# Two-phase depthwise convolution with three half filters, in a two-layer trunk on one core

## The chip, the cores and the metric

The kernel runs on one core of one Trainium2 chip. The metric is the device time of one execution in microseconds (us). The profile names the engines PE (TensorE, matmul; PEld is its weight load), DVE (VectorE), ACT (ScalarE), POOL (GpSimd) and SP (SyncE, which issues the DMAs).

## The reference

Two layers of a trunk with 128 context tokens and 512 latent tokens (640 in all), width 1024. A layer normalises x, modulates it by a vector c (one for the context, one for the latent tokens), projects it to four groups of heads, mixes each group over the tokens (differential attention "da", latent attention "mla", neighbourhood attention "na", a Conformer convolution), projects back, adds, and then does the same around an MLP of 4096. The group that matters here:

```python
def conformer_conv(u, dw, db, ln_g, ln_b):
    a, b = jnp.split(u, 2, axis=-1)
    g = a * jax.nn.sigmoid(b)
    y = lax.conv_general_dilated(g, dw[:, None, :], window_strides=(1,),
                                 padding=[(CONV_W // 2, CONV_W // 2)], ...
                                 feature_group_count=CONV_CH) + db
    return jax.nn.silu(layernorm(y, ln_g, ln_b))

def modulation(cvec, w_mod, b_mod):
    m = jax.nn.silu(cvec) @ w_mod + b_mod
```

CONV_W is 31, CONV_CH is 256: each of 256 channels has its own filter of 31 taps along the tokens. The layernorm behind it runs over the 256 channels. The modulation is a product of a vector with a 1024 x 6144 matrix, for two vectors and two layers.

## The kernel before

**Number format.** Everything is float32. A matmul is made of three (mm3, L242 to L246): operands are split into a high part (rounded, by ACT, L192) and a low part (the rest, by POOL or DVE, L193), and high x high, high x low and low x high are summed in PSUM. So each weight granule costs splits on ACT and POOL before PE can use it. POOL takes its instructions in order.

**Memory.** The transposed x, the weights and all scratch lie in regions of one SBUF tile (`fa`), addressed by name. Two regions matter: "conv" (10,960 bytes a partition: the padded inputs g and the outputs y of the convolution, in two halves of 128 channels) and "c" (8192 bytes: the vectors silu(c) spread over all partitions, the row form `cb`, which VectorE needs when it computes modulation products itself). PSUM has two single banks g (`gb`) and three double ones s (`sb`).

**Stages.** start() loads x, computes silu(c), builds the row form of c by 16 PE transposes (L1223) and four DVE copies out of PSUM (L1241), sums the squares of x (L1235), computes layer 0's first modulation by dot products on PE (L1263), and runs the convolution's input projection as the normalised x arrives (L1284, L1289). Then, in each layer: the na value projection, na queries and keys, the da value projection (in_v, 40 groups of three matmuls of 288 columns, 120 in all), and a pipeline of 60 attention units (20 na, 20 da, 20 mla) with the other projections in between. The MLP follows (ff); during it VectorE computes the next layer's modulation from `cb` (mod_dot, L301).

**The convolution.** conv_evac writes g (L520 through a transposing view: the latent tokens are stored by grid column; L523 for the context). g is a row of 700 elements: 512 latent and 128 context tokens with zeros between. conv_taps (L413) makes 31 DVE instructions over 670 elements for each half: L419 multiplies by tap 0 and adds the bias, L423 multiplies by tap j and adds. They are background jobs: each has a price in ns (450 or 780), each piece of the program brings a credit (fill, L253), and when the credit covers the first job it is written into the program there. What is left is written out at attention unit DR = 2 (drain). Behind the last tap stands the chain conv_finish (L431): the sum of the two halves on POOL (L438), three ticks later a matmul with ones on PE (L443, mean over the channels), the subtraction of the mean on DVE (L446), squares on ACT (L451), their sum on POOL (L452), six ticks later again ones, and so on. A tick is a step of the program text: prices and ticks decide in which place of each engine's queue the instruction stands, not when it runs.

Of the kernel before, what the change touches and what calls it, by code (L numbers as in the profile page):

```python
# [11 lines left out]
AF = mybir.ActivationFunctionType  # L12
ALU = mybir.AluOpType
# [3 lines left out]
T = 640  # L17
# [11 lines left out]
C_BMOD, C_GMIX, C_GFF, C_DW, C_DB = 0, 48, 56, 64, 126  # L29
# [40 lines left out]
BGP = (100,100,100,100,100)  # L70
# [2 lines left out]
XPOS = 8  # L73
LEADF = (2,3,4,5,6,7)
YOUT = ((2,4,6,8),(2,4,6,8))
CB = "DDDD"
KINDS = ("D", "D")
ROWS = (1,1,0,0)
END = object()
# [3 lines left out]
class Builder:  # L83
# [310 lines left out]


    def conv_g(self, c):
        return self.F("conv", 2800 * c, 700)

    def conv_y(self, c):
        return self.F("conv", 5600 + 2680 * c, 670)  # L400

    def conv_zero(self):
        for c in range(2):
            g = self.conv_g(c)
            for a, b in ((0, 15), (527, 557), (685, 700)):
                self.nc.gpsimd.memset(g[:, a:b], 0.0)

    def conv_cols(self, l):
        nc = self.nc
        nc.vector.tensor_scalar(out=self.F("dwh", 0, 62), in0=self.col(l, C_DW, 62), scalar1=0.5, scalar2=None, op0=ALU.mult)  # L410
        nc.vector.tensor_scalar(out=self.F("lnh", 0, 4), in0=self.col(l, C_LNG, 4), scalar1=0.5, scalar2=None, op0=ALU.mult)

    def conv_taps(self, l, c):  # L413
        nc = self.nc
        g, y = self.conv_g(c), self.conv_y(c)
        dwh = self.F("dwh", 0, 2, 31)

        def first():
            nc.vector.tensor_scalar(out=y, in0=g[:, 0:670], scalar1=dwh[:, c, 0:1],  # L419
                                    scalar2=self.col(l, C_DB + c), op0=ALU.mult, op1=ALU.add)  # L420

        def tap(j):
            nc.vector.scalar_tensor_tensor(out=y, in0=g[:, j:j + 670], scalar=dwh[:, c, j:j + 1],  # L423
                                           in1=y, op0=ALU.mult, op1=ALU.add)
        self.bg.append((450, first, BGP[l]))
        for j in range(1, 31):
            self.bg.append((780, lambda j=j: tap(j), BGP[l]))
        if c == 1:
            self.bg.append((0, lambda: self.chain(self.conv_finish(l, (self.R("oa", 0, 2, T), self.R("oa", 5120, 2, T)))), 0))

# [77 lines left out]
    def conv_evac(self, l, c, part):  # L508
        nc = self.nc

        def evac(h, ps):
            t0, t1 = HALF[h]
            if part == "b":
                self.tabled(nc.scalar.activation(self.F("conv", 5600 + 2680 * c, T)[:, t0:t1], ps[:, 0:t1 - t0], AF.Tanh, scale=0.5))
                return
            th = self.F("conv", 5600 + 2680 * c, T)
            g = self.conv_g(c)
            nl = min(t1, NLAT) - t0
            out = g[:, 15:527].rearrange("p (r w) -> p w r", r=8)[:, t0 // 8:(t0 + nl) // 8]
            nc.vector.scalar_tensor_tensor(out=out, in0=th[:, t0:t0 + nl].rearrange("p (w r) -> p w r", r=8), scalar=1.0,  # L520
                                           in1=ps[:, 0:nl].rearrange("p (w r) -> p w r", r=8), op0=ALU.add, op1=ALU.mult)
            if t1 > NLAT:
                nc.vector.scalar_tensor_tensor(out=g[:, 557:685], in0=th[:, 512:640], scalar=1.0,  # L523
                                               in1=ps[:, nl:t1 - t0], op0=ALU.add, op1=ALU.mult)
                self.conv_taps(l, c)
        return evac
# [658 lines left out]
    def start(self):  # L1185
        nc, d = self.nc, self.d
        self.table(TABLE_TANH)
        ct = self.F("sq", 0, 8, 2)
        nc.sync.dma_start(ct, d["ct"])
        nc.scalar.dma_start(self.F("ident", 0, 256), d["cst"][:, 1024:1280])  # L1190
        for l in range(L):
# [1 line left out]
        ring = [self._view(self.at, 4096 * s, (1024,)) for s in range(4)] + [self.F("e", 4096 * s, 1024) for s in range(3)]  # L1193
        ring += [self.R(r, a, 1024) for r, a in (("oa", 4096), ("ob", 0), ("ob", 4096))]
        rows = [self.F("conv", 1024 * s, 256) for s in range(2)]
        self.ct, self.sel = ct, self.F("sq", 64, 2)
        sel = self.sel
        js = [w * 8 + k for k in range(8) for w in (SC1, SH1)]
        n = len(ring)
        self.ng = 4  # L1200
# [8 lines left out]
        for _ in range(4):  # L1209
# [5 lines left out]
                                       op0=ALU.add, op1=ALU.mult)  # L1215
        th = self.small(4 * 4).rearrange("p (a b) -> p a b", b=2)
# [1 line left out]
        self.table(TABLE_LN)  # L1218
        nc.vector.tensor_scalar(out=th, in0=th, scalar1=0.5, scalar2=0.5, op0=ALU.mult, op1=ALU.add)
        nc.vector.tensor_tensor(out=ct, in0=ct, in1=th, op=ALU.mult)  # L1220
        for v in range(2):
            for k in range(8):
                nc.tensor.transpose(self.sb[1 + v][:, k * 128:k * 128 + 128], ct[:, k, v:v + 1].to_broadcast([128, 128]), self.ident)  # L1223
        seq = ((0, 0, NLAT), (1, NLAT, T))
        ps = [self.gb[1][:, 0:NLAT], self.sb[0][:, 0:T - NLAT]]
        first = 0 if SUMS[0] == "D" else 1
        bufs = [self.F(*p, T) for p in (("tmp", 0), ("tmp", 3072), ("mla", 6144), ("conv", 8192))]
        for k in range(8):
            sq = bufs[k % 4]
# [3 lines left out]
            if k % 2 or SUMS[k // 2] == "D":  # L1233
                for v, a, b in seq:
                    nc.tensor.matmul(ps[v], self.ones, sq[:, a:b], start=k == first, stop=k == 7)  # L1235
        for v in range(2):
            for j, a in enumerate((0, 512)):
                if CB[2 * v + j] == "A":
                    nc.scalar.copy(self.cb[:, v, a:a + 512], self.sb[1 + v][:, a:a + 512])
                else:  # L1240
                    nc.vector.tensor_copy(self.cb[:, v, a:a + 512], self.sb[1 + v][:, a:a + 512])  # L1241
        for v, a, b in seq:
            self.rsq(self.rn[:, a:b], ps[v], 1.0 / 1024)
        pm = self.gb[0][:, 0:32].rearrange("p (a b) -> p a b", b=2)
# [2 lines left out]
        ws = [self.w_get(128) for _ in range(4)]  # L1247
# [73 lines left out]
        for i in range(4):  # L1321
# [2 lines left out]
            self.w_done()  # L1324
            evs[i](1, acb[i])
        self.table(TABLE_LN)

    def mod_rows(self, l, whichs):

# [74 lines left out]
    def mix(self, l):  # L1404
        nc, d = self.nc, self.d
        if l == 0:
            self.start()
        else:
            self.conv_zero()
            self.conv_cols(l)  # L1410
            self.in_conv(l, self.lead)
        self.swap(l, "bt")
        self.lam(l)
        for kind in range(3):
            self.na_bias_load(l, 0, kind)
        self.in_v(l, "na")
        for p in range(2):
            nc.sync.dma_start(self.qk_k("na", p)[:, 512:640], d["cnak"][l, :, p])
            self.mtile(self.na_evac(l, p, "q"))
            self.mtile(self.na_evac(l, p, "k"))  # L1420
        self.finish_chains()
        self.edge_load(0)
        self.edge_load(1)
        self.in_v(l, "da")
        self.ring = self.gb

        def rest():
            for p in range(2):
                nc.sync.dma_start(self.qk_k("da", p)[:, 512:640], d["cdak"][l, :, p])
                yield from self.pieces(self.da_evac(l, p, "q"))  # L1430
                yield from self.pieces(self.da_evac(l, p, "k"))
            yield from self.in_mla(l)
        plan = [(PL[0], PL[1], rest(), 14), (PL[15], PL[16], self.out_pieces(l, ["oa"], 2, 4), 16), (PL[3], PL[4], self.kv_up(l), 10), (PL[5], PL[6], self.out_pieces(l, ["ob"], 2, 4), 16),
                (PL[7], PL[8], self.q_up(l), 10), (PL[9], PL[10], self.out_pieces(l, ["oa"], 2, 4), 16),
                (PL[13], PL[14], self.ff_lead(l), 8)]
        hooks = {PL[2]: lambda: self.da_cut(1), PL[11]: lambda: self.chain(self.da_stack(1, 0)),
                 PL[12]: lambda: self.chain(self.da_stack(1, 1))}
        hooks[DR] = self.drain
        hooks[60] = lambda: self.swap(l, "we")
        self.out, self.out_n, self.norm_a = self.out_pieces(l, ["ob"], 2, 4, last=True), 0, self.norm(l, 1, 0)  # L1440
        plan = [[0, 0, *p] for p in plan]
        for t in self.pipeline(l, hooks):
            for job in [j for j in plan if t >= j[2]]:
                done, pos, t0, t1, gen, n = job
                if pos == 0 and t0 == PL[9]:
                    self.finish_chains("da")
                pos += 1
                while done < n and done * (t1 - t0) * 3 < pos * n:
                    next(gen)
                    done += 1  # L1450
                job[:2] = done, pos
# [244 lines left out]
```

## Time and profile before

| | |
|---|---|
| median of 3 runs (lowest to highest) | 1734.57 us (1733.45 to 1736.35) |
| profiled execution | 1735.52 us, span 1733.6 us |
| PE, DVE, ACT, POOL busy in the span | 96%, 62%, 43%, 38% |

The span runs from the first to the last instruction of the profiled execution. The trace allows a look at each instruction's start, duration and, where an engine stood idle ahead of it, what released it ("[8.73 <-POOL ra L193]": idle for 8.73 us until POOL's L193 had written ra).

### The profile page before, as it was taken

The numbers are of one execution on the slowest core, as the hardware profiler recorded it, in microseconds if no ns is written. First come the engines' busy times: TensorE is split into PE (matmuls) and PEld (weight loads), VectorE is DVE, ScalarE is ACT, GpSimd is POOL, SyncE is SP. The second block draws the span as 40 slices with busy tenths as digits, with TensorE's granted clock in tenths as the row PEclk, the third lists the DMA queues.
The fourth block names the chain that finished last, engine by engine and source line by source line (L and its number), as shares of the span: only waits on it lengthen the run. The fifth ranks groups of instructions, "written<-read, shape, count | busy, mean of one in ns | idle before, by whom it ended". The sixth has DMA issues, their size and how long they took to land. (4 is left out here: it accounts for less than half of the span.)

```text
span 1733.6 us, 29318 instructions
## 1 busy us (share of the span) xinstructions
PE 1664.6 (96%) x11368; PEld 1570.3 (91%) x11368; DVE 1083.0 (62%) x2136; ACT 740.7 (43%) x1655; POOL 656.5 (38%) x527
## 2 busy tenths in 40 slices
PE   7999999999989999999999899999999999999997
PEld 5869988788889999999999888887989999999997
DVE  4772448868988887876377933886784333333335
ACT  4323666756423332222343247776563322332322
POOL 0225533305344455544324364332343333333330
PEclk8999999999989999999999999999999999999999
DMA  9563244202355454443222222430113222222221
GB/s 367 185 202 106 75 110 101 63 14 86 110 160 167 147 158 147 152 153 111 73 71 71 64 86 84 108 88 20 50 39 97 73 74 74 80 79 74 74 62 61
DMA packets 62331, 178.28 MB, mean 103 GB/s; under 512 B 8656, under 2 KB 20048, under 8 KB 62192
## 3 DMA queue, kind: packets, MB, share of 16 engines
q1 hardware_dynamic: 61984, 176.14, 33.0%
q8 instruction: 89, 1.46, 0.3%
q14 instruction: 50, 0.41, 0.1%
q10 hardware_dynamic: 144, 0.13, 0.0%
q0 software_dynamic: 64, 0.14, 0.0%
HBM read 158.52 MB, written 3.83 MB: 94 GB/s over the span
## 5 line engine op out<-in xcount | busy, mean ns | idle before, releaser
L193 POOL TENSOR_TENSOR ra<-fa,ra 128x512 fp32r<-128x512 f32 (+1 forms) x239 | 345.7, 1459 | 545.2 <-ACT ra L192 524.5
L193 POOL TENSOR_TENSOR we<-fa,we 128x512 fp32r<-128x512 f32 x126 | 188.8, 1510 | 275.2 <-ACT we L192 253.5
L1077 DVE TENSOR_TENSOR fr<-fr 128x384 f32<-128x384 f32 (+1 forms) x128 | 103.9, 814 | 273.7 <-ACT or L1076 150.6
L192 ACT CAST ra<-fa 128x512 fp32r<-128x512 f32 (+1 forms) x240 | 147.2, 621 | 255.1 <-PE s L245 163.7
L244 PE MATMUL s<-ra 128*128 128x256 f32 (+2 forms) x600 | 185.4, 309 | 8.3 <-DVE fa L392 7.6
L245 PE MATMUL s<-ra 128*128 128x256 f32 (+2 forms) x600 | 184.3, 307 | 0.0
L246 PE MATMUL s<-ra 128*128 128x256 f32 (+2 forms) x600 | 184.1, 307 | 0.0
L301 DVE CUSTOM_DVE_ANT_0 fa<-fa 128x1024 f32<-128x1024 f32 x112 | 173.2, 1546 | 0.2
L392 DVE SCALAR_TENSOR_TENSOR fa<-s,fa 128x128 f32<-128x128 f32 (+1 forms) x310 | 121.3, 427 | 74.8 <-PE s L246 74.8
L246 PE MATMUL g<-ra 128*128 128x384 f32 (+2 forms) x508 | 158.3, 312 | 8.7 <-POOL ra L193 8.7
L244 PE MATMUL g<-ra 128*128 128x384 f32 (+2 forms) x508 | 162.2, 319 | 2.5 <-DVE bt L1010 1.9
L245 PE MATMUL s<-ra,we 128*128 128x384 f32 (+1 forms) x480 | 152.1, 317 | 12.0 <-DVE ra L370 12.0
L245 PE MATMUL g<-ra 128*128 128x384 f32 (+2 forms) x508 | 157.8, 311 | 0.8 <-POOL ra L193 0.8
L192 ACT CAST we<-fa 128x512 fp32r<-128x512 f32 x132 | 81.2, 620 | 175.2 <-PE s L245 127.9
L246 PE MATMUL s<-ra,we 128*128 128x384 f32 (+1 forms) x480 | 150.1, 313 | 0.0
L244 PE MATMUL s<-ra,we 128*128 128x384 f32 (+1 forms) x480 | 148.8, 314 | 0.8 <-DVE fa L520 0.8
L392 DVE SCALAR_TENSOR_TENSOR fa<-g,fa 128x128 f32<-128x128 f32 (+1 forms) x266 | 109.3, 441 | 40.4 <-PE g L246 39.0
L244 PEld LDWEIGHTS s<-ra 128*128 128x128 f32 x600 | 115.6, 193 | 17.6 <-DVE fa L392 7.9
L423 DVE SCALAR_TENSOR_TENSOR fa<-fa 128x670 f32<-128x670 f32 x120 | 124.1, 1098 | 0.5
L697 PE MATMUL g<-at 128*128 128x128 f32 x848 | 116.9, 277 | 2.8 <-DVE fa L392 1.5
L245 PEld LDWEIGHTS s<-ra 128*128 128x128 f32 x600 | 115.9, 193 | 4.0 <-issue 4.0
L246 PEld LDWEIGHTS s<-ra 128*128 128x128 f32 x600 | 115.8, 193 | 3.6 <-issue 3.6
(299 smaller groups left out, 4484.4 us busy)
## 6 DMA issues: line engine op xcount, KB each, us to landing
fa<-in_wg SPq DMA_DIRECT2D x187, 512.0 KB, 3.6
fa<-in_wmod SPq DMA_DIRECT2D x73, 512.0 KB, 4.2
at<-in_wmod SPq DMA_DIRECT2D x20, 512.0 KB, 6.5
ra<-ra SPq DMA_DIRECT2D x64, 96.0 KB, 2.2
ra<-ra SPq DMA_DIRECT2D x64, 80.0 KB, 2.3
fa<-in_nab SPq DMA_DIRECT2D x24, 192.0 KB, 3.7
fa<-in_xT SPq DMA_DIRECT2D x8, 320.0 KB, 5.9
os<-in_wmod SPq DMA_DIRECT2D x3, 512.0 KB, 10.2
```

The source lines that it names most:

```text
L192: nc.scalar.copy(hi, src)
L193: (lo_eng or nc.gpsimd).tensor_tensor(out=lo, in0=src, in1=hi.bitcast(F32), op=ALU.subtract)
L244: nc.tensor.matmul(out, a[0], b[0], start=start, stop=False)
L245: nc.tensor.matmul(out, a[0], b[1], start=False, stop=False)
L246: nc.tensor.matmul(out, a[1], b[0], start=False, stop=stop)
L301: self.nc.vector.tensor_tensor_reduce(out=self.junk, in0=slot, in1=self.cb[:, v], scale=1.0, scalar=0.0, op0=ALU.mult, op1=ALU.add, accum_ ...
L392: self.mark = nc.vector.scalar_tensor_tensor(out=xs, in0=ps[:, a - t0:b - t0], scalar=self.mod(l, v, which)[:, m:m + 1], in1=xs, op0=ALU.m ...
L423: nc.vector.scalar_tensor_tensor(out=y, in0=g[:, j:j + 670], scalar=dwh[:, c, j:j + 1], in1=y, op0=ALU.mult, op1=ALU.add)
L697: self.nc.tensor.matmul(u["o"], v[:, p * 128:p * 128 + 128] if v.shape[1] > 128 else v, u["pt"][:, b * 128:b * 128 + 128], start=b == 0, s ...
L1077: nc.vector.tensor_tensor(out=r, in0=r, in1=r, op=ALU.mult)
```

## The change

A convolution with 31 taps at even and odd positions is written with three half filters. For a half of the channels g is read in two phases, the words 0, 2, 4, ... (ph[0]) and 1, 3, 5, ... (ph[1]). The 16 even taps run over ph[0] into a_ (336 elements), the 15 odd taps over ph[1] into b_ (335), and 16 taps with the sums of neighbouring coefficients (`both`, and the last even tap alone) run over u = ph[1] + ph[0] shifted, into r, from which b_ is taken away at once. The outputs at even places are a_ + b_ + bias, those at odd places r + bias less a_ shifted. That makes 50 instructions of half the length for each half of the channels instead of 31, priced 350 (300 for a plain multiplication). y is written in the place of g. The even and odd taps read with a step of two words, the two combinations write with one; the taps on u read adjacent words.

The scratch u, r, b_ and `both` lies in region "c", where `cb` stood from the start on. So the row form of c is no longer built in start(): a new function c_rows does it at attention unit 41 of layer 0's pipeline, through the banks g. `ct` (silu(c) by columns) moves into the same region's end, a PSUM tile is cleared on DVE at the start, and conv_cols has one more addition per layer (the sums of neighbouring coefficients).

```diff
     def conv_g(self, c):
-        return self.F("conv", 2800 * c, 700)
+        return self.F("conv", 5344 + 2808 * c, 702)
     def conv_y(self, c):
-        return self.F("conv", 5600 + 2680 * c, 670)
+        return self.conv_g(c)[:, 0:670]
...
     def conv_taps(self, l, c):
         nc = self.nc
-        g, y = self.conv_g(c), self.conv_y(c)
...
-        self.bg.append((450, first, BGP[l]))
-        for j in range(1, 31):
-            self.bg.append((780, lambda j=j: tap(j), BGP[l]))
+        g, y, w, both = self.conv_g(c), self.conv_y(c), self.F("dwh", 0, 2, 31)[:, c], self.F("c", 5376, 2, 15)[:, c]
+        ph = [g[:, a:a + 701:2] for a in range(2)]
+        a_, u, r, b_ = (self.F("conv", 2560 * c, 336), self.F("c", 0, 350), self.F("c", 1408, 335),
+                        self.F("c", 2752 + 1344 * c, 335))
+        bias = self.col(l, C_DB + c)
...
+                    job(350, nc.vector.scalar_tensor_tensor, out=out, in0=src[:, i:i + n], scalar=x, op0=ALU.mult, **kw)
+                else:
+                    job(300, nc.vector.tensor_scalar, out=out, in0=src[:, 0:n], scalar1=x, scalar2=None, op0=ALU.mult)
+        even, odd = ([w[:, j:j + 1] for j in range(a, 31, 2)] for a in range(2))
+        job(350, nc.vector.tensor_tensor, out=u, in0=ph[1][:, 0:350], in1=ph[0][:, 1:351], op=ALU.add)
+        taps(a_, ph[0], even, 336)
+        taps(b_, ph[1], odd, 335)
+        taps(r, u, [both[:, j:j + 1] for j in range(15)] + [even[15]], 335, in1=b_, op1=ALU.subtract)
+        job(350, nc.vector.scalar_tensor_tensor, out=y[:, 0:670:2], in0=a_[:, 0:335], scalar=bias, in1=b_, op0=ALU.add, op1=ALU.add)
+        job(350, nc.vector.scalar_tensor_tensor, out=y[:, 1:670:2], in0=r, scalar=bias, in1=a_[:, 1:336], op0=ALU.add, op1=ALU.subtract)
...
-        ct = self.F("sq", 0, 8, 2)
+        ct = self.F("c", 7168, 8, 2)
...
+        nc.vector.memset(self.sb[2], 0.0)
...
-        for v in range(2):
-            for k in range(8):
-                nc.tensor.transpose(self.sb[1 + v][:, k * 128:k * 128 + 128], ct[:, k, v:v + 1].to_broadcast([128, 128]), self.ident)
...
+    def c_rows(self):
+
+        for v in range(2):
+            for b in range(2):
+                ps = self.g()
+                for k in range(4):
+                    self.nc.tensor.transpose(ps[:, k * 128:k * 128 + 128],
+                                             self.ct[:, 4 * b + k, v:v + 1].to_broadcast([128, 128]), self.ident)
+                self.nc.vector.tensor_copy(self.cb[:, v, 512 * b:512 * b + 512], ps)
...
+        if l == 0:
+            hooks[41] = self.c_rows
```

Lines of the changed kernel have other numbers: L243 to L245 are its L244 to L246, L192 its L193, L455 is the first ones matmul (L443 before), L458 the subtraction of the mean (L446), L778 the first maximum of an na unit (L766), L698, L709, L809 and L810 the turning, the value products and the scores of the mla units (L686, L697, L797, L798), L1338 the transposes of c_rows.

PE's order in layer 1, before, where the first ones matmul (L443) stands: row 5629, behind the output projection's matmuls of 384 columns.

```order
L244 MATMUL g_64<-ra 128x384
L245 MATMUL g_64<-ra 128x384
L246 MATMUL g_64<-ra 128x384
L443 MATMUL g_63<-fa 128x512
L686 MATMUL s_65<-fa 128x128
L686 MATMUL s_66<-fa 128x128 x3
L443 MATMUL g_64<-fa 128x128
L756 MATMUL s_65<-bt_8172 128x128
```

PE's order in layer 1 now, around the same ones matmul (L455): row 5463, among the 120 matmuls of 288 columns of the da value projection (`ra` holds the split x and weights, `fa` the sum of the two halves).

```order
L243 MATMUL s_65<-ra 128x288
L244 MATMUL s_65<-ra 128x288
L245 MATMUL s_65<-ra 128x288
L455 MATMUL s_66<-fa 128x512
L455 MATMUL s_67<-fa 128x128
L243 MATMUL g_64<-ra 128x288
L244 MATMUL g_64<-ra 128x288
L245 MATMUL g_64<-ra 128x288
```

The two ones matmuls moved from behind the first na units to behind the 90th of the 120 value matmuls; in layer 0 they moved likewise, from row 824 to row 665, behind the 102nd.

DVE's order in layer 1, before, from the last write of g to the first na unit.

```order
L520 SCALAR_TENSOR_TENSOR fa<-fa,s_67 128x16x8
L523 SCALAR_TENSOR_TENSOR fa<-fa,s_67 128x128
L419 TENSOR_SCALAR fa<-fa 128x670 x2
L423 SCALAR_TENSOR_TENSOR fa<-fa 128x670 x60
L766 ISA s_66,fa<-s_66,fa 128x384
L766 ISA fa 128x1
L488 STREAM_SHUFFLE fa<-s_65 32x256
```

DVE's order in layer 1 now, from the second half's last taps to the first na unit; L458 subtracts the mean.

```order
L423 TENSOR_TENSOR fa<-fa 128x350
L423 SCALAR_TENSOR_TENSOR fa<-fa 128x336
L423 SCALAR_TENSOR_TENSOR fa<-fa 128x335 x32
L458 SCALAR_TENSOR_TENSOR fa<-s_66,fa 128x512
L458 SCALAR_TENSOR_TENSOR fa<-s_67,fa 128x128
L778 ISA s_66,fa<-s_66,fa 128x384
L778 ISA fa 128x1
L500 STREAM_SHUFFLE fa<-s_65 32x256
```

The subtraction of the mean (four instructions, of which two are shown; the second half's two are alike) now stands between the last tap and the first maximum.

PE's order among layer 0's mla units, before.

```order
L697 MATMUL g_63<-at_81 128x128 x5
L797 MATMUL s_65<-bt_636 128x512
L798 MATMUL s_65<-bt_636 128x128
L686 MATMUL s_66<-fa 128x128 x5
L697 MATMUL g_64<-at_81 128x128
L686 MATMUL s_67<-fa 128x128 x5
```

The same place now, with the four groups of four transposes of c_rows (L1338).

```order
L709 MATMUL g_63<-at_81 128x128 x5
L1338 MATMUL g_64<-fa 128x128 x4
L809 MATMUL s_65<-bt_618 128x512
L1338 MATMUL g_63<-fa 128x128 x4
L1338 MATMUL g_64<-fa 128x128 x4
L810 MATMUL s_65<-bt_618 128x128
L698 MATMUL s_66<-fa 128x128 x2
L1338 MATMUL g_63<-fa 128x128 x4
L698 MATMUL s_66<-fa 128x128 x3
L709 MATMUL g_64<-at_81 128x128
```

Sixteen transposes came in between the scores, the turning and the value products, on the banks g that the value products use.

## Rows read from the trace of the kernel before

**Rows 1.** The page, table of busy time: us, share, instructions.

```profile
PE 1664.6 (96%) x11368; PEld 1570.3 (91%) x11368; DVE 1083.0 (62%) x2136; ACT 740.7 (43%) x1655; POOL 656.5 (38%) x527
```

**Rows 2.** PE's waits: engine, line, releaser; us, times, longest.

```profile
PE g L246 <- POOL ra L193: 8.7, 1, 8.7
```

**Rows 3.** DVE's timeline: start us, us, engine line op, tiles, xcount.

```profile
418.69 0.61 DVE L377 SCALAR_TENSOR_TENSOR fa<-fa 128x384 f32<-128x384 f32 x1
419.22 0.61 DVE L370 SCALAR_TENSOR_TENSOR ra<-fa,ra 128x384 fp32r<-128x384 f32 x1
...
929.44 2.14 DVE L419 TENSOR_SCALAR fa<-fa 128x670 f32<-128x670 f32 x2
931.49 64.21 DVE L423 SCALAR_TENSOR_TENSOR fa<-fa 128x670 f32<-128x670 f32 x60
...
931.49 4.21 DVE L423 SCALAR_TENSOR_TENSOR fa<-fa 128x670 f32<-128x670 f32 x5
```

**Rows 4.** POOL's timeline, layer 1.

```profile
970.86 3.85 POOL L193 TENSOR_TENSOR ra<-fa,ra 128x512 fp32r<-128x512 f32 x2 [3.18 <-ACT ra L192]
...
995.78 1.37 POOL L438 TENSOR_TENSOR fa<-fa 128x670 f32<-128x670 f32 x1 [14.04 <-DVE fa L423]
```

**Rows 5.** PE's timeline around the hole of layer 1.

```profile
989.35 0.34 PE L245 MATMUL g<-ra 128*128 128x384 f32 x1
998.43 0.69 PE L246 MATMUL g<-ra 128*128 128x384 f32 x1 [8.73 <-POOL ra L193]
...
1001.79 0.52 PE L244 MATMUL g<-ra 128*128 128x384 f32 x1
...
1002.51 0.33 PE L244 MATMUL g<-ra 128*128 128x384 f32 x1
```

**Rows 6.** Windows: us, busy of PE, PEld, DVE, ACT, POOL (x), PEclk, DMA.

```profile
345.00:355.00 10.00, 9.74 (x66) 7.65 (x65) 6.13 (x13) 7.52 (x19) 0.00 (x0) 1.00 0.08 29
990.00:1000.00 10.00, 1.57 (x5) 1.58 (x6) 7.96 (x16) 1.29 (x3) 4.22 (x4) 0.60 0.00 0
```

**Rows 7.** DVE's timeline, behind the last tap of layer 0.

```profile
136.24 0.20 DVE L410 TENSOR_SCALAR fa<-fa 128x62 f32<-128x62 f32 x1
```

**Rows 8.** PE's timeline in the da value projections.

```profile
153.22 0.30 PE L246 MATMUL s<-ra 128*128 128x288 f32 x1
...
983.42 0.29 PE L244 MATMUL s<-ra 128*128 128x288 f32 x1
```

**Rows 9.** Line L423 in 964.6 to 972: ns min/median/max.

```profile
L423 DVE SCALAR_TENSOR_TENSOR fa<-fa x7: 902/907/1945, 964.6 to 971.6; 128x670 f32<-128x670 f32 x7
```

**Rows 10.** DVE's timeline at the start.

```profile
7.48 1.28 DVE L1241 COPY fa<-s 128x512 f32<-128x512 f32 x2
...
19.32 2.49 DVE L193 TENSOR_TENSOR wes<-fa,wes 128x512 fp32r<-128x512 f32 x4
```

**Rows 11.** DVE's groups by form: count, busy us, mean ns, idle before.

```profile
L392 DVE SCALAR_TENSOR_TENSOR fa<-s,fa 128x128 f32<-128x128 f32 x214 | 63.5, 344 | 43.6 <-PE s L246 43.6
...
L392 DVE SCALAR_TENSOR_TENSOR fa<-s,fa 128x384 f32<-128x384 f32 x96 | 57.8, 613 | 31.2 <-PE s L246 31.2
...
L520 DVE SCALAR_TENSOR_TENSOR fa<-fa,s 128x384 f32<-128x384 f32 x3 | 2.5, 835 | 1.5 <-ACT fa L514 1.5
...
L520 DVE SCALAR_TENSOR_TENSOR fa<-fa,s 128x128 f32<-128x128 f32 x3 | 1.1, 380 | 11.8 <-ACT fa L514 9.8 <-PE s L246 2.0
```

**Rows 12.** PE's timeline among layer 0's mla units.

```profile
346.18 0.73 PE L686 MATMUL s<-fa 128*128 128x128 f32 x5 [0.26 <-DVE fa L716]
...
350.03 0.71 PE L686 MATMUL s<-fa 128*128 128x128 f32 x5
```

**Rows 13.** PE's timeline at the start.

```profile
5.20 3.67 PE L1223 MATMUL s<-fa 128*128 128x128 f32 x16 [5.20 <-DVE fa L1182]
...
22.39 0.69 PE L244 MATMUL s<-ra,wes 128*128 128x384 f32 x1 [4.54 <-ACT ra L1284]
```

More of the change, by code (lines that the diff above doesn't have):

```diff
@@ L75 @@
 YOUT = ((2,4,6,8),(2,4,6,8))
-CB = "DDDD"
 KINDS = ("D", "D")
@@ L404, in conv_zero @@
             g = self.conv_g(c)
-            for a, b in ((0, 15), (527, 557), (685, 700)):
+            for a, b in ((0, 15), (527, 557), (685, 702)):
                 self.nc.gpsimd.memset(g[:, a:b], 0.0)
@@ L410, in conv_cols @@
         nc.vector.tensor_scalar(out=self.F("dwh", 0, 62), in0=self.col(l, C_DW, 62), scalar1=0.5, scalar2=None, op0=ALU.mult)
+        w = self.F("dwh", 0, 2, 31)
+        nc.vector.tensor_tensor(out=self.F("c", 5376, 2, 15), in0=w[:, :, 0:30:2], in1=w[:, :, 1:31:2], op=ALU.add)
         nc.vector.tensor_scalar(out=self.F("lnh", 0, 4), in0=self.col(l, C_LNG, 4), scalar1=0.5, scalar2=None, op0=ALU.mult)
@@ L414, in conv_taps, with job, taps @@
         nc = self.nc
-        g, y = self.conv_g(c), self.conv_y(c)
[L416 to L424, printed above, removed]
-        self.bg.append((450, first, BGP[l]))
-        for j in range(1, 31):
-            self.bg.append((780, lambda j=j: tap(j), BGP[l]))
+        g, y, w, both = self.conv_g(c), self.conv_y(c), self.F("dwh", 0, 2, 31)[:, c], self.F("c", 5376, 2, 15)[:, c]
[3 more added lines that the diff above has]
+        bias = self.col(l, C_DB + c)
+        def job(ns, f, *args, **kw):
+            self.bg.append((ns, lambda: f(*args, **kw), BGP[l]))
+        def taps(out, src, ws, n, **kw):
+            for i, x in enumerate(ws):
+                if i or not kw:
+                    kw = {"in1": out, "op1": ALU.add} if i else {}
+                if kw:
+                    job(350, nc.vector.scalar_tensor_tensor, out=out, in0=src[:, i:i + n], scalar=x, op0=ALU.mult, **kw)
[8 more added lines that the diff above has]
+        job(350, nc.vector.scalar_tensor_tensor, out=y[:, 1:670:2], in0=r, scalar=bias, in1=a_[:, 1:336], op0=ALU.add, op1=ALU.subtract)
         if c == 1:
@@ L513, in evac @@
             if part == "b":
-                self.tabled(nc.scalar.activation(self.F("conv", 5600 + 2680 * c, T)[:, t0:t1], ps[:, 0:t1 - t0], AF.Tanh, scale=0.5))
+                self.tabled(nc.scalar.activation(self.F("conv", 2560 * c, T)[:, t0:t1], ps[:, 0:t1 - t0], AF.Tanh, scale=0.5))
                 return
-            th = self.F("conv", 5600 + 2680 * c, T)
+            th = self.F("conv", 2560 * c, T)
             g = self.conv_g(c)
@@ L1195, in start @@
         rows = [self.F("conv", 1024 * s, 256) for s in range(2)]
-        self.ct, self.sel = ct, self.F("sq", 64, 2)
+        self.ct, self.sel = ct, self.F("c", 7232, 2)
         sel = self.sel
+        nc.vector.memset(self.sb[2], 0.0)
         js = [w * 8 + k for k in range(8) for w in (SC1, SH1)]
@@ L1235, in start @@
                     nc.tensor.matmul(ps[v], self.ones, sq[:, a:b], start=k == first, stop=k == 7)
[L1236 to L1241, printed above, removed]
         for v, a, b in seq:
```

## The prediction

> **What bounds the kernel now.** I read the page's table of busy time first: TensorE (PE) is busy 96% of the span, VectorE (DVE) 62% [rows 1], so a DVE instruction saved is worth nothing by itself. It pays only where PE stands still for it. So the list of PE's waits came next. Its longest single piece is 8.7 us, PE waiting for a split on GpSimd (POOL, L193) [rows 2]. That wait is the convolution of layer 1 in disguise. In DVE's timeline two L419 and sixty L423 run without a gap from 929.44 to 995.7 [rows 3]. POOL, idle for 14.04 us, starts the sum of the two channel halves (L438) at 995.78 when the last tap is done, and only behind it, since its queue is in order, the split that PE wants [rows 4]. PE stops at about 989.7 and resumes at 998.43, with matmuls of 0.52 us instead of 0.33 until 1002 [rows 5]. The window 990:1000 shows the hole: 1.57 us of PE, granted clock 0.60 [rows 6]. Layer 0 has no such hole: its last tap ends at 136.2 [rows 7], and PE is still in its value projection at 153.2 [rows 8]. So the change can gain or lose in three places: layer 1's hole, the start (which transposes and copies leave), and layer 0's attention (where they arrive).
>
> **The taps of layer 1.** Undisturbed, five L423 take 4.21 us, each 0.907 long, so one follows another after (4.21 − 0.907)/4 = 0.826 us, for 670 elements [rows 3, 9]. For 384 an L377 starts at 418.69 and its successor at 419.22: 0.53 [rows 3]. The slope is (0.826 − 0.53)/286 = 1.035 ns an element, so 335 elements cost 0.53 − 49 × 0.001035 = 0.479: half the elements, 58% of the time. An addition of 350 is 0.43, by the start's four splits of 512 in 2.49 us, 0.60 apart [rows 10]. A layer has had 62 operations, 62 × 0.826 = 51.2 us undisturbed. It gets 98 of the half length and two additions: 46.9 + 0.9 = 47.8. A quarter of the multiplications goes, but 38 more fixed costs of 0.13 come, and 3.4 us are left. In fact the taps of layer 1 took 66.3 us. The other 15.1 are POOL's: beside its splits a tap takes up to 1.945 us [rows 9], and a pair of splits 3.85 [rows 4]. There are sixteen splits beside the taps (eight pairs like the two shown), 0.94 us lost for each. The order keeps the same eighteen splits ahead of the sum on POOL, so I carry the 15.1 over. Taps end at 929.4 + 47.8 + 15.1 = 992.3 instead of 995.7; the sum of the halves (1.37 us) ends at 993.8.
>
> **The place of the chain.** This is where the gain is lost. The jobs of a half were priced 450 + 30 × 780 and now about 17,400 together, so the list runs dry earlier in the program, and the chain behind the last tap moves with it. The ones matmul that reads the sum stood in row 5629 of PE's order, past the hole; it now stands in row 5463, behind the 90th of 120 matmuls of the da value projection. PE passed that place at 983.4 [rows 8]. There it will wait for the sum until 993.8: 10.4 us instead of 8.7, with 6.3 us of work (983.4 to 989.7) behind the wait instead of ahead of it. That is +1.7 us. Queued behind the waiting matmul on PE are the last 30 value matmuls, the first na scores and the output projection; nothing else can feed PE. On DVE four mean subtractions now stand ahead of the first na maximum, about 2 us by the 0.613 and 0.344 of L392 for 384 and 128 elements [rows 11]; PE has over 6 us of matmuls meanwhile, so I put them at nothing, and at 2 us without that cover. On POOL two splits instead of four follow the sum directly, and PE needs the first 6 us later than it did. The clock: from 998.43 to 1001.79 eleven matmuls went 0.305 apart [rows 5], half of that lost, 1.7 us; what a longer stop adds lies between 0 and as much again, and I take 0.3. Layer 1: +2.0.
>
> **Layer 0's taps** gain the same 3.4 us on DVE, and there the ones matmul moves up to the 102nd value matmul, at 153.2 [rows 8]. Taps that ended 17 us earlier still do: 0.
>
> **c_rows.** Sixteen transposes land in the first mla units of layer 0, near 344 us, where PE is busy 9.74 of 10 us [rows 6]. Five of the same form (L686) take 0.71 there, 0.11 apart [rows 12]: 16 × 0.11 = 1.8 us. They share the two banks g with the value products, and their third and fourth group wait for copies of 0.64 us (1.28 for two, [rows 10]) on a DVE that also runs the softmax, busy 61% [rows 6]. The trace has no row for that wait: between nothing and 1.7 (two copies, and a softmax step in front) I take 0.5, the nearest row being the 0.26 that PE waits for DVE in these units already [rows 12]. PE is the bound here, so nothing hides it: +2.3.
>
> **The start.** The sixteen transposes took PE 3.67 us, 0.22 apart where L686 has 0.11, so at half clock [rows 12, 13]; the four copies took DVE twice 1.28 [rows 10]. Without them the sums may start earlier, but on a PE that has done nothing before and then runs them at that half clock. What is late behind them are the first splits: PE waits 4.54 us for L1284 until 22.39 [rows 13]. In the new order four DVE splits stand ahead of the first normalisation (2.49 us), while half of the second set of dot products comes ahead of the first convolution matmul. Between −2.5 (all copies gained) and +2.5 (all four splits in front) I take +0.3. The memset of one PSUM tile lies where DVE has nothing yet, and the addition of 30 columns is one small operation a layer: 0.
>
> **Sum.** 2.0 + 0 + 2.3 + 0.3 = +4.6 us. On the profiled run's 1735.5 that is 1740.1; that run lies 0.9 over the median of the runs shown, 1734.6, and against the median I forecast 1739.2.
>
> **A rule against the change.** Even and odd taps read every second word, and the combinations write every second word. No row of before does either. The nearest is L520, which writes 64 words apart: 0.380 us for 128 elements and 0.835 for 384, 1.78 ns an element, against 1.05 for L392 (0.344, 0.613) [rows 11]. The Trainium skill, "Vector Engine (DVE) Microarchitecture Reference", § 5.2 Measured stream behaviour on trn2, says that a port streams at full rate only over runs of two or more adjacent words, and gives 1.73 ns a column where one source hops at every element; for writes L520 agrees. The Trainium skill, "SBUF — State Buffer", § Door 1, says instead that two hits in a 16-byte line are enough, which every second word gives; L520 has one hit in a line and so doesn't decide between the two.
>
> **Rivals.**
> Strided operands pay as L520 does. Per layer 68 operations (31 taps, the addition and two combinations in each half) × 335 × 0.73 ns = 16.6 us. In layer 1 they lengthen the stop directly: 1739.2 + 16.6 = 1755.8. Layer 0 still hides them: 136.2 − 3.4 + 16.6 = 149.4, the sum at 150.8, ahead of 153.2. For it: L520. Against: its words lie 256 bytes apart, these eight. At a third of the price it is 1744.7. Chance 0.15.
>
> The taps end early enough (not slower). If, with even and odd chains alternating, the next starts after the 0.07 of an addition (0.60 less 512 × 0.001035) rather than 0.13, then 98 × 0.418 + 0.9 + 15.1 = 57.0 and the taps end at 986.4; if short operations lose only half of the 15.1 to POOL, at 984.8. The stop falls to 4.5 or 2.9 us, and layer 1 gives −4.2 − 1.0 or −5.8 − 1.7 in place of +2.0: 1732.0 or 1729.7, about 1731. It decides where the taps end before 988.4. Against: taps of L423 hang on one another and L377 on nothing before it, yet one slope and one fixed cost fit both. Chance 0.17.
>
> The edits cancel. The start gives back its copies (−2.5), the transposes fall partly into waits (+1.8), layer 1 ends at +1.0: 1734.9. For it: the copies do stand among the additions that the sums wait for. Chance 0.18.
>
> **Chances.** The forecast's own case, +2 to +8, has 0.50. What a measurement of this kernel can tell from no change is about 0.2%, 3.5 us: below 1731.1 is faster, above 1738.0 slower. Faster is over half of the second rival and a little of the third, 0.14. The same is a third of the forecast's case, most of the third rival and the rest of the second, 0.39. Slower is left with 0.47. The range is 1731.0 to 1752.0; its own case alone is 1736.5 to 1742.5.
>
> **What would show it.** A tap of 335 after 0.48 us, strided or not (0.72 would be the first rival); taps of layer 1 ending near 992; one wait of PE at L455 of about 10 us in place of the 8.7 at L246, beginning near 983 and followed by half clock; sixteen transposes near 344 and PE's later stages some 2 us later; no wait in layer 0. The forecast is wrong if layer 1's taps end before 988, or if PE waits over 15 us at L455.

## The result, and the profile after

The changed kernel takes 1745.57 us (median of 4 runs, 1745.34 to 1746.36) against 1735.46 us before (median of 4 runs, 1733.45 to 1737.44): a ratio of 1.0059, 95% interval 1.0042 to 1.0077. It is 10.1 us slower. The forecast was 1739.2 and slower; the loss is twice its size, and it sits at another place.

PE's waits after (us in total, times, longest), two of the list:

```profile
PE g L245 <- POOL ra L192: 18.7, 1, 18.7
...
PE g L1245 <- DVE fa L1242: 7.2, 1, 7.2
```

The 8.7 us that PE waited for a split of POOL [rows 2] have become 18.7, and no wait at the ones matmul (L455) is in the list. POOL's timeline of layer 1 shows why (start, us, instruction, count, idle time ahead of it):

```profile
927.98 2.67 POOL L192 TENSOR_TENSOR ra<-fa,ra 128x512 fp32r<-128x512 f32 x2 [3.19 <-ACT ra L191]
936.03 30.68 POOL L192 TENSOR_TENSOR ra<-fa,ra 128x512 fp32r<-128x512 f32 x4 [5.39 <-ACT ra L191]
...
984.65 3.02 POOL L192 TENSOR_TENSOR ra<-fa,ra 128x512 fp32r<-128x512 f32 x2 [4.23 <-ACT ra L191]
...
1001.30 1.37 POOL L450 TENSOR_TENSOR fa<-fa 128x670 f32<-128x670 f32 x1
```

Four splits that took 3.85 us a pair before [rows 4] take 30.68 together, of which the first alone takes 26.17 (the last section has its row). DVE's timeline over the same time:

```profile
927.65 0.53 DVE L423 TENSOR_TENSOR fa<-fa 128x350 f32<-128x350 f32 x1
...
931.24 13.49 DVE L423 SCALAR_TENSOR_TENSOR fa<-fa 128x336 f32<-128x336 f32 x28
944.65 0.39 DVE L423 TENSOR_SCALAR fa<-fa 128x336 f32<-128x336 f32 x1
944.96 14.92 DVE L423 SCALAR_TENSOR_TENSOR fa<-fa 128x335 f32<-128x335 f32 x31
959.79 0.39 DVE L423 TENSOR_SCALAR fa<-fa 128x335 f32<-128x335 f32 x1
960.09 0.56 DVE L423 SCALAR_TENSOR_TENSOR fa<-fa 128x335 f32<-128x335 f32 x1
960.57 0.52 DVE L423 TENSOR_TENSOR fa<-fa 128x350 f32<-128x350 f32 x1
961.00 28.84 DVE L423 SCALAR_TENSOR_TENSOR fa<-fa 128x336 f32<-128x336 f32 x33
1005.37 1.69 DVE L458 SCALAR_TENSOR_TENSOR fa<-s,fa 128x512 f32<-128x512 f32 x4 [15.52 <-PE s L455]
```

From 931.24 to 961 the taps run as if POOL were not there: 28 in 13.49 us, the last 0.56 long, is (13.49 − 0.56)/27 = 0.479 each. Only the last 33 are slowed (28.84 us), by POOL and because from 964 on nearly every tap hangs on the one before it. They end at 989.8. So the taps are done 5.9 us earlier than before [rows 3], 1.8 of it because they begin earlier (927.65, not 929.44), and POOL has paid for it. PE, which needs the splits, stands still:

```profile
943.19 0.34 PE L244 MATMUL g<-ra 128*128 128x384 f32 x1
962.26 0.69 PE L245 MATMUL g<-ra 128*128 128x384 f32 x1 [18.73 <-POOL ra L192]
...
1004.23 1.24 PE L455 MATMUL s<-fa 128*128 128x512 f32 x4
```

and the windows around it (us; busy of PE, PEld, DVE, ACT, POOL; granted clock; DMA) show 0.00 us of PE in 950:960 and a granted clock of 0.50, the level of 1.2 GHz, after PE had stood still since 943.5; before, the hole had 1.57 us of PE in 10 [rows 6]:

```profile
950.00:960.00 10.00, 0.00 (x0) 0.00 (x0) 10.00 (x22) 0.00 (x0) 10.00 (x1) 0.50 0.00 0
960.00:970.00 10.00, 7.74 (x37) 7.74 (x37) 9.75 (x12) 0.61 (x2) 6.71 (x4) 0.65 0.42 104
```

By the time that PE comes to the ones matmul, at 1004.23, the sum of the halves is done, since 1002.67.

How the 10 us come together is read from the same instruction in both traces. First PE rows after, of the start, of the first mla scores and of c_rows:

```profile
7.16 2.07 PE L1245 MATMUL g<-fa 128*128 128x512 f32 x2 [7.16 <-DVE fa L1242]
...
22.98 0.69 PE L243 MATMUL s<-ra,wes 128*128 128x384 f32 x1 [1.67 <-ACT ra L1288]
...
336.08 1.02 PE L809 MATMUL s<-bt 96*128 96x512 f32 x2
...
341.85 0.60 PE L1338 MATMUL g<-fa 128*128 128x128 f32 x4
...
343.47 1.09 PE L1338 MATMUL g<-fa 128*128 128x128 f32 x8 [0.16 <-ACT fa L714]
...
344.98 0.65 PE L1338 MATMUL g<-fa 128*128 128x128 f32 x4
...
416.06 0.81 PE L352 MATMUL s<-fa 128*128 128x384 f32 x2
```

Then two of them in the trace of before:

```profile
338.13 1.02 PE L797 MATMUL s<-bt 96*128 96x512 f32 x2
...
415.87 0.81 PE L353 MATMUL g<-fa 128*128 128x384 f32 x2
```

At the first mla scores the changed kernel is 2.05 us ahead, behind the mla units 0.19 late: the start gave 2.05, and c_rows took 2.24. The hole of layer 1 adds 18.73 − 8.73 = 10.0. Half clock follows both holes (0.50 in 962:965 here, matmuls 0.305 apart before [rows 5]), so the two about cancel. The spans differ by 1743.5 − 1733.6 = 9.9.

### The profile page after: what moved, and what is told of

It is laid out like the page before. It is cut to its first block, busy times and chain, and to the rows that moved or that the text cites. A ratio compares the mean times of both kernels' runs of the same rounds, so it can differ in the third digit from the quotient of the medians.

```text
span 1743.5 us, 29400 instructions
## 1 busy us (share of the span) xinstructions
PE 1660.0 (95%) x11368; PEld 1567.0 (90%) x11368; DVE 1078.3 (62%) x2215; ACT 741.4 (43%) x1655; POOL 675.5 (39%) x527
## 5 line engine op out<-in xcount | busy, mean ns | idle before, releaser
L192 POOL TENSOR_TENSOR ra<-fa,ra 128x512 fp32r<-128x512 f32 (+1 forms) x239 | 365.0, 1540 | 537.9 <-ACT ra L191 521.8
L192 POOL TENSOR_TENSOR we<-fa,we 128x512 fp32r<-128x512 f32 x126 | 187.6, 1500 | 288.4 <-ACT we L191 266.5
L243 PE MATMUL s<-ra 128*128 128x256 f32 (+2 forms) x600 | 184.1, 307 | 1.3 <-DVE fa L1192 0.7
L244 PE MATMUL s<-ra 128*128 128x256 f32 (+2 forms) x600 | 182.7, 304 | 0.8 <-POOL ra L192 0.8
L245 PE MATMUL s<-ra 128*128 128x256 f32 (+2 forms) x600 | 182.8, 305 | 0.0
L245 PE MATMUL g<-ra 128*128 128x256 f32 (+2 forms) x508 | 157.9, 311 | 18.7 <-POOL ra L192 18.7
L243 PE MATMUL g<-ra 128*128 128x256 f32 (+2 forms) x508 | 162.3, 319 | 1.9 <-DVE bt L1022 1.9
L244 PE MATMUL s<-ra,we 128*128 128x384 f32 (+1 forms) x464 | 148.2, 320 | 12.5 <-DVE ra L369 12.5
L244 PE MATMUL g<-ra 128*128 128x256 f32 (+2 forms) x508 | 157.8, 311 | 0.0
L245 PE MATMUL s<-ra,we 128*128 128x384 f32 (+1 forms) x464 | 146.3, 315 | 0.0
L243 PE MATMUL s<-ra,we 128*128 128x384 f32 (+1 forms) x464 | 144.6, 316 | 0.3 <-ACT fa L336 0.2
L243 PEld LDWEIGHTS s<-ra 128*128 128x128 f32 x600 | 113.7, 190 | 10.5 <-issue 6.5
L709 PE MATMUL g<-at 128*128 128x128 f32 x848 | 116.7, 277 | 2.8 <-DVE fa L391 1.6
L245 PEld LDWEIGHTS s<-ra 128*128 128x128 f32 x600 | 113.7, 190 | 4.6 <-issue 4.6
L244 PEld LDWEIGHTS s<-ra 128*128 128x128 f32 x600 | 113.8, 190 | 3.1 <-issue 2.1
L423 DVE SCALAR_TENSOR_TENSOR fa<-fa 128x335 f32<-128x335 f32 (+1 forms) x188 | 115.1, 663 | 2.0
```

Of the source, the lines that this page charges most:

```text
L192: (lo_eng or nc.gpsimd).tensor_tensor(out=lo, in0=src, in1=hi.bitcast(F32), op=ALU.subtract)
L423: self.bg.append((ns, lambda: f(*args, **kw), BGP[l]))
L709: self.nc.tensor.matmul(u["o"], v[:, p * 128:p * 128 + 128] if v.shape[1] > 128 else v, u["pt"][:, b * 128:b * 128 + 128], start=b == 0, s ...
```

## The experiments

Lines are those of each kernel and differ by a few from the changed kernel's. All times are medians; ratios are against the kernel before, run on the same chip.

**A gap for POOL.** Behind every fourth tap of a half, a memset of one column, pinned between its taps (EVERY is 4):

```diff
+                prev[1] += 1
+                if prev[1] % EVERY == 0:
+                    prev[0] = nc.vector.memset(self.F("c", 6000 + 8 * c, 1), 0.0)
+                    self.after(prev[0], i)
```

> Change: behind every fourth tap of a half, one memset of a single column on DVE, which reads nothing; nothing else. Theory A (POOL's split that started at 936.03 could not read SBUF for 26 us because DVE ran instructions with two SBUF operands without a gap): the memset opens a gap, POOL's pair takes about 3 us as before, PE's wait of 18.7 us at L245 for POOL goes; taps then end near 993 and PE waits some 10 to 13 us at the ones matmul instead, about 1738 us. Rival B (POOL's 26 us came from something else, such as a late operand of the split): the 18.7 us stay, 1746 to 1748 us, some 2 us more for 24 memsets.

Measured 1742.52 us, 1.0034 (1.0021 to 1.0047). POOL's split, PE's wait and the sum of the halves in that run:

```profile
935.69 3.06 POOL L193 TENSOR_TENSOR ra<-fa,ra 128x512 fp32r<-128x512 f32 x2 [5.40 <-ACT ra L192]
```

```profile
PE s L467 <- POOL fa L462: 15.3, 1, 15.3
```

```profile
996.81 1.37 POOL L462 TENSOR_TENSOR fa<-fa 128x670 f32<-128x670 f32 x1 [16.49 <-DVE fa L427]
```

The pair takes 3.06 us instead of being held for 26, and the wait for a split is gone. In its place stands the wait that the prediction had put there, at the ones matmul (L467 here). It is longer than the 10.4 us forecast, 15.3, since the taps end at 996.7 and not at 992.3. So theory A holds, with a higher price for what follows: 1742.5 us, not about 1738.

**Splits on DVE.** The condition that picks DVE for a split gets `self.tapping`, true from where layer 1's taps are put on the list of jobs to the sum of the halves:

```diff
-... self.nc.vector if n < 4 and CUT[n * 2 + j] == "D" or ...
+... self.nc.vector if self.tapping or n < 4 and CUT[n * 2 + j] == "D" or ...
```

> Change: while layer 1's taps are pending, the low parts of the weights (the splits) are made on DVE between the taps, not on POOL. Theory A: no split waits for the shared read port; DVE pays 16 to 18 times 0.60 us instead of losing 0.94 to each of POOL's, taps end near 986, PE waits 4 to 6 us at the ones matmul and nowhere else in this stage: about 1730 us. Rival B (POOL was not the cause): PE still waits about 18 us for a split, 1745 us or more. Rival C (splits on DVE stand behind taps and wait for ACT's casts): several PE waits of 1 to 3 us each for DVE, 1735 to 1740 us.

Measured 1733.54 us, 0.9985 (0.9976 to 0.9994). PE's waits in 900:1030, and two DVE rows of that run:

```profile
PE s L458 <- POOL fa L453: 3.4, 1, 3.4
PE s L771 <- ACT at L707: 2.3, 1, 2.3
```

```profile
976.65 1.28 DVE L193 TENSOR_TENSOR ra<-fa,ra 128x512 fp32r<-128x512 f32 x2
977.86 11.58 DVE L425 SCALAR_TENSOR_TENSOR fa<-fa 128x335 f32<-128x335 f32 x16
```

Two splits cost DVE 1.28 us; beside POOL's they had cost it 0.94 each and POOL half again its time. Of 18.7 us waiting 3.4 are left. The time is 3.5 us over what theory A gave, and the taps end at 989.4, not near 986; 2.3 us are a new wait of an na unit for ACT. The sixteen taps in 11.58 us, 0.73 each, ran beside two splits of POOL, which were written past the end of the list and so were not moved.

**The place alone.** Prices 480 and 405 in place of 350 and 300, so that the ones matmul stands in row 5607:

```diff
-        job(350, ...
+        job(480, ...
```

> Change: prices of the background jobs 480 and 405 instead of 350 and 300, so that a half costs about 23,900 as it did before the change; the chain behind the taps moves back in PE's order from row 5463 to about row 5607. Theory A (the loss is POOL's starved split, whose taps on DVE stand in the same order): PE's wait of about 18 us stays, 1744 to 1747 us. Rival D, the prediction's step (the earlier place of the ones matmul makes PE wait): some 5 to 10 us less, 1736 to 1740 us.

Measured 1746.90 us, 1.0065 (1.0047 to 1.0083); PE's wait and POOL's row:

```profile
PE g L245 <- POOL ra L192: 18.9, 1, 18.9
```

```profile
935.48 30.67 POOL L192 TENSOR_TENSOR ra<-fa,ra 128x512 fp32r<-128x512 f32 x4 [5.40 <-ACT ra L191]
```

The place is worth nothing while POOL is held: the hole is upstream of it. D falls for the changed kernel as it stands.

**The place, with the gap.** Both of these edits together.

> Change: the memset behind every fourth tap (first experiment) and prices of 480 and 405 (third), so that POOL is not held off and the ones matmul stands in row 5607. This isolates the prediction's step of the place: against the first experiment (PE waits 15.3 us at the ones matmul, 1742.5) PE waits 9 to 10 us, later, for a split behind the sum of halves: 1736 to 1738 us. Rival K (the place is worth nothing): 1742 us.

Measured 1738.62 us, 1.0011 (1.0002 to 1.0021). PE waits 10.7 us for a split behind the sum, not 15.3 at the ones matmul:

```profile
PE g L246 <- POOL ra L193: 10.7, 1, 10.7
```

Against the first experiment that is 3.9 us less. So the place does cost, some 4 us, once the other hole is out of the way. K falls.

**The move of the row form.** The kernel before, with c_rows in the place of the transposes and copies of the start; the cells of c are used again by another stage in between, so its row form holds other values, and only its time is read.

```diff
-                nc.tensor.transpose(self.sb[1 + v][:, k * 128:k * 128 + 128], ...
...
+            hooks[41] = self.c_rows
```

> Change: the kernel before, with its 31 taps, and of the change only the row form of c moved from the start to attention unit 41 of layer 0 (with the memset of a PSUM tile). Theory A (the move gives about 2 us at the start and takes about 2 us in the mla units, the loss is in the taps): 1734.5 to 1737 us. Rival E, the prediction's term of +2.3 with +0.3 for the start: 1738 us. Rival F (the move is the whole loss): 1745 us.

Measured 1736.20 us, 0.9999 (0.9989 to 1.0008). The first mla scores and the row behind the mla units:

```profile
335.66 1.02 PE L797 MATMUL s<-bt 96*128 96x512 f32 x2
...
415.61 0.81 PE L353 MATMUL s<-fa 128*128 128x384 f32 x2
```

2.47 us ahead, then 0.26 ahead: the gain of the start pays for c_rows. E and F fall; the loss is in the taps, within the 1.7 us or so that this interval leaves open.

**The moment of the request.** POOL's request at 936.03 came just as a tap started. One DVE operation of 110 elements more shifts all taps:

```diff
+        if l == 1 and c == 0:
+            job(0, nc.vector.scalar_tensor_tensor, out=self.F("c", 5600, SHIFT), in0=u[:, 0:SHIFT], scalar=w[:, 0:1], ...
```

> Change: one more DVE instruction in all, a scalar-tensor operation of 110 elements (about 0.24 us, its result is not used) behind the first addition of layer 1's taps, so that all later taps start about half a tap later against POOL's and ACT's work. Theory G (whether POOL's request gets the port between two gap-free taps hangs on the moment at which it comes): the split at 936.0 is no longer held for 26 us, PE's 18.7 us at L245 go or shrink to a few us, PE waits at the ones matmul as with the memsets: 1738 to 1743 us. Rival H (short gap-free taps always hold POOL off): the 18.7 us stay, 1745 to 1747 us.

Measured 1747.41 us, 1.0061 (1.0044 to 1.0078):

```profile
PE g L246 <- POOL ra L193: 19.0, 1, 19.0
```

The request now came half a tap later, at 936.74, and was held as long, 26.4 us. G falls, as far as one shift can tell.

**Short or strided.** The kernel before with each L423 cut into two of 335 adjacent columns, price 390:

```diff
+            for t in (0, 335):
+                self.bg.append((390, lambda j=j, t=t: tap(j, t), BGP[l]))
```

> Change: the kernel before, its 31 taps kept, but each tap behind the first cut into two instructions over the left and the right 335 columns (120 short instructions in layer 1, all over adjacent words, four of them independent of one another), at half the price each. What holds POOL off in the changed kernel? Theory L (short independent taps without a gap, whatever their step): a split of POOL is held for tens of us, PE waits 20 to 45 us for it, 1750 to 1780 us. Rival S (the step of two words is what holds POOL off): POOL's pairs take about 3 us as before, taps take 120 x 0.479 + 16 = 74 us, the hole grows by 8 us, 1742 to 1746 us.

Measured 1780.77 us, 1.026 (1.023 to 1.029). POOL, PE's wait, and DVE's group of the taps (count, busy us, mean ns):

```profile
943.00 57.39 POOL L193 TENSOR_TENSOR ra<-fa,ra 128x512 fp32r<-128x512 f32 x4 [5.19 <-ACT ra L192]
```

```profile
PE s L246 <- POOL ra L193: 46.3, 1, 46.3
```

```profile
L423 DVE SCALAR_TENSOR_TENSOR fa<-fa 128x335 f32<-128x335 f32 x120 | 57.5, 554 | 0.0
```

The same convolution, no word strided, only shorter instructions: POOL is held until the last tap is done, and the taps lose nothing to it. The wait of 46.3 us and the time are just above the ranges of theory L. S falls.

**One chain.** The changed kernel with each tap pinned behind the one written before it (`self.after(i, self.tap)` in job).

> Change: the changed kernel with the DVE order of the taps pinned to the order in which they are written (even, then odd, then the sums, the first half, then the second), so that nearly every tap hangs on the one before it and the odd taps no longer alternate with the even ones. Theory M (a tap that must wait for the one before leaves POOL a way in, as in the last sixteen taps of the changed kernel, 0.605 apart): no split is held, PE's 18.7 us at L245 go; but taps 0.605 apart take 96 x 0.605 + 2 + 16 = 76 us, end near 1003 and PE waits 15 to 20 us later, for the sum of halves: 1742 to 1748 us in all. Rival L2 (shortness alone holds POOL off, dependent or not): the wait at L245 stays at 18 us or more and another comes behind it, over 1755 us.

Measured 1751.16 us, 1.0089 (1.0060 to 1.0119):

```profile
935.45 3.09 POOL L193 TENSOR_TENSOR ra<-fa,ra 128x512 fp32r<-128x512 f32 x2 [5.40 <-ACT ra L192]
```

```profile
PE s L461 <- POOL fa L456: 18.5, 1, 18.5
```

Taps that hang on one another leave a way in: the pair takes 3.09 us. The price is a later end, and the 18.5 us at the ones matmul come to nearly what the starved split had cost; the total is 3 us over what M gave, 2.1 of them in a wait of an na unit for ACT. L2 falls.

**Both repairs.** Splits on DVE and the prices of 480 and 405, with the half filters:

> Change: splits on DVE while layer 1's taps are pending (as in the second experiment) and prices of 480 and 405 (as in the third). Theory A with the prediction's step of the place: with taps ending near 989 and the ones matmul in row 5607 PE no longer waits for the convolution at all, the 3.4 us of the second experiment and its half clock go: 1728 to 1731 us. Rival I (the time is given back in the attention units, since the chain behind the taps is late for the output projection, or ACT's softmax is late): 1733 us as in the second experiment.

and the splits on DVE alone, with the old taps:

> Change: the kernel before, with its 31 taps, and only the splits of layer 1 on DVE while taps are pending. Theory A (what costs is the port that taps and splits share; the half filters are worth only their 3.4 us): taps end near 991, the hole shrinks from 8.7 to 4 or 5 us, 1730 to 1733 us, so most of the gain of the second experiment is had with the old taps. Rival J (the half filters are needed for it): 1735 us or more.

Measured 1725.30 us, 0.9937 (0.9922 to 0.9952), and 1724.50 us, 0.9933 (0.9918 to 0.9948). The windows of the first, then of the second:

```profile
980.00:1000.00 20.00, 20.00 (x136) 19.09 (x135) 16.64 (x40) 9.70 (x27) 7.69 (x9) 1.00 0.36 111
```

```profile
980.00:1000.00 20.00, 20.00 (x142) 18.89 (x141) 19.70 (x36) 8.52 (x24) 5.75 (x6) 1.00 0.31 98
```

In both PE is busy throughout at a granted clock of 1.00 (2.4 GHz): the hole is closed, also with the old taps, for which I had still expected 4 or 5 us of it. The two times cannot be told apart, and both lie below every range given (1728 to 1731, and 1730 to 1733). The half filters leave DVE more room (16.64 us busy instead of 19.70), but nothing waits for it. Both beat the kernel before by over 10 us.

With the old taps the reason is not the one that theory A gave. The taps do not end near 991 there but after 1000, 5 us later than before, and the sum of the halves with them. What changed is the order. In the kernel before, four splits stood behind the sum in POOL's queue, and PE's hole lasted until the first of them was done:

```profile
997.11 4.96 POOL L193 TENSOR_TENSOR ra<-fa,ra 128x512 fp32r<-128x512 f32 x4
```

The same four (the same places in the list of all splits) with the old taps and the splits on DVE, and the sum:

```profile
985.66 1.29 DVE L194 TENSOR_TENSOR ra<-fa,ra 128x512 fp32r<-128x512 f32 x2
990.55 1.29 DVE L194 TENSOR_TENSOR ra<-fa,ra 128x512 fp32r<-128x512 f32 x2
...
1000.93 1.69 POOL L441 TENSOR_TENSOR fa<-fa 128x670 f32<-128x670 f32 x1 [2.29 <-DVE fa L425]
```

They are made 9 to 11 us earlier, ahead of the last four taps, and on DVE work of the attention units (from 991.77) comes between those taps too. So a late end of the taps no longer holds PE. No run moves these four alone, so how much of the gain is due to the port and how much to the order is not shown.

## Why the prediction was right and wrong

The forecast of slower holds, and the time lies in the range, though above the 1736.5 to 1742.5 of the forecast's own case. The sum does not hold: +4.6 us forecast, +10.1 measured. That it came out slower is in part luck. With the start and c_rows as measured (−2.05 and +2.24) and layer 1 as forecast (+2.0) the sum is +2.2, which the prediction itself would have called no change; the rest came from a wait that it doesn't have.

**The step that failed** is "The order keeps the same eighteen splits ahead of the sum on POOL, so I carry the 15.1 over." I had read the contention of [rows 4, 9] as a price that DVE pays for each split. It is a question of who gets the port, and it came out the other way: while short taps ran without a gap, DVE lost nothing and POOL stood for 26 us. The Trainium skill, "SBUF — State Buffer", § Who interferes with whom, says that a DVE instruction with two SBUF inputs contends with a GpSimd instruction that reads SBUF, and that the pair of ports that they share is an exclusive lock. The traces agree with the exclusion: a tap beside a split took 1.945 us, not 0.907 [rows 9], and a split beside taps 26.17, not 1.3. What is shown here besides, and decides, is that DVE can go first dozens of times in a row.

**The taps.** 0.479 us for 335, strided or not, was right, and the first rival falls: 28 strided taps (even and odd alternating) ran 0.479 apart, the cut taps over adjacent words took 554 ns each like the changed kernel's 0.56. Of the two rules of the Trainium skill that were weighed, that of "SBUF — State Buffer", § Door 1, is the one with which the trace agrees at a step of two words of four bytes (0.479 us for 335); the 1.73 ns a column of "Vector Engine (DVE) Microarchitecture Reference", § 5.2, did not appear.

**The place of the chain** was right as a mechanism and without effect as a cause. It costs 3.9 us, shown only where POOL was let in. The sum's +2.0 is net of the taps' 3.4; its own figures give the place 5.1, a wait of 10.4 us at the new place against 8.7 − 3.4 = 5.3 at the old one. The end of the taps was put too early there as well. The first experiment's taps begin at 927.3, and 47.8 us undisturbed make 975.1. Sixteen instructions beside splits come 1.48 apart instead of 0.479, 16.0 us more (15.1 in the sum). And 43 taps come 0.603 apart, as taps do that hang on their forerunner: 5.3 us more, for which the sum has nothing. That is 996.4 of 996.7. The memsets add next to nothing: four such taps with one among them are followed by the next 2.41 us later, which is 4 × 0.603.

```profile
983.74 2.38 DVE L427 SCALAR_TENSOR_TENSOR fa<-fa 128x335 f32<-128x335 f32 x4
986.07 0.06 DVE L433 MEMSET fa<- 128x1 f32 x1
986.15 2.38 DVE L427 SCALAR_TENSOR_TENSOR fa<-fa 128x335 f32<-128x335 f32 x4
```

The order would have told me of them: towards the end of the list nothing independent is left to alternate with.

**c_rows** was right: +2.24 against +2.3. **The start** was wrong, −2.05 against +0.3. The sums begin at 7.16 and their first pair takes 2.07 us, where the pair at 13.75 takes 1.02, as feared. (That this and the transposes before ran at half clock shows in their spacing alone; the windows there, 7:9 now and 5:9 before, read a granted clock of 1.00.) The four splits that I had charged do cost: DVE's first normalisation starts at 20.17, not 18.39, and the first matmul that needs it at 22.98, 0.59 later than before [rows 13]. PE's wait there is 1.67 us and not 4.54 because sixteen of the dot products now stand ahead of it (L1267, at 20.29). The gain comes behind that: those sixteen are out of the way, and the granted clock, 0.50 (1.2 GHz) in 26:30 in both kernels after PE's waits, is 0.79 in 30:34 where it was 0.65. How the 2.05 divide between the two is not worked out. **Layer 0** was right: its taps end 6.6 us earlier (1.2 of it because they begin earlier, at 64.01 and not 65.23), and PE gains nothing by it.

```profile
129.63 0.19 DVE L409 TENSOR_SCALAR fa<-fa 128x62 f32<-128x62 f32 x1
```

**The rival of the early taps** did not come true: the taps ended at 989.8, not before the 988.4 from which it was to decide. They came that close not because taps start sooner behind one another (0.479 apart) but by starving the engine that feeds PE: 12 of their instructions stood beside splits, not sixteen.

Two things stay open. Why pairs of splits beside operations of 336 at 66 and at 928 us got in, within 1.6 us a split, was not tried; at 928 the operations beside them are multiplications by a scalar alone and the last writes of g, at 66 they are ordinary taps, and at 95.91, still in layer 0, a pair took 6.60 us. And why taps of 670 let POOL in at every turn in layer 1, and gap-free ones of 335 do not: the kernels that held POOL for long, strided and adjacent, share the short taps that need not wait for their forerunner; what in the arbitration makes the difference is not shown.

## What to carry to other kernels

A contention price belongs to the lengths and gaps at which it was measured; where a change makes one side's instructions shorter, forecast both that it keeps losing and that it now starves the other, and see who feeds the bound engine. Where two engines fight for one port over a small task, giving the task to the engine that otherwise loses time to it can be cheaper than either: 0.64 us a split on DVE against 0.94 lost to each of POOL's. And before making an engine faster, ask whether what waits at its end could be moved: PE waited for splits that stood behind the sum of the halves in an in-order queue. The old taps with the splits of one stage in another queue gained 11 us, though they ended later, and the new taps added nothing to that.

## What the hardware showed that was not expected

A split of POOL, 1.3 us alone, was held for 26.2 us by taps of 335 and 336 with two SBUF operands. The line's durations in 935:962 (ns, least, median, longest):

```profile
L192 POOL TENSOR_TENSOR ra<-fa,ra x1: 26174/26174/26174, 936.0 to 936.0; 128x512 fp32r<-128x512 f32 x1
```

In the kernel with cut taps one took 53.7 us of the 57.39 shown:

```profile
L193 POOL TENSOR_TENSOR ra<-fa,ra x2: 1270/27482/53694, 943.0 to 996.6; 128x512 fp32r<-128x512 f32 x2
```

Multiplications by a scalar in between (0.39 us) did not let it in. A memset of one column (0.06 us) did, and so did taps that hang on one another, five of them here in 2.98 us, 0.60 apart (DVE after):

```profile
967.11 2.98 DVE L423 SCALAR_TENSOR_TENSOR fa<-fa 128x335 f32<-128x335 f32 x5
```

In each of the three kernels with half filters in which a split was held, the hold ended behind the same instruction, the second half's addition (TENSOR_TENSOR of 350, at 960.57 in the changed kernel): 936.03 + 26.17 less the 1.3 of the split itself is 960.9. In "The place alone" and "The moment of the request" it ended at 960.5 and 961.9, with the addition at 960.19 and 961.53. DVE's next operation starts 0.43 us after the addition, which lasts 0.52, so no gap shows there; what the addition and the memset have that the taps have not is not shown.
